# Attention stage of a diffusion block: bias and half of the rotary on GpSimd, softmax's small steps for two heads at once, a pair's scores three projection steps later

## The chip, the core and the metric

The program runs on one core of one Trainium2 chip. The metric is the device time of one execution in microseconds (us), the median of several runs. The engines are TensorE (PE; its weight loads are PEld), VectorE (DVE), ScalarE (ACT), GpSimd (POOL), and SyncE (SP), which issues all transfers. Each engine works through its own list of instructions in order.

## The reference

Two layers over 512 latent tokens (an 8 x 64 grid) and 256 context tokens, model width 1024, eight attention heads of 64. Cut to what the change touches:

```python
p, u, vs, q, k, v, gl = split(a @ w_in[l])            # one projection for everything
q, k = apply_rope(to_heads(q)), apply_rope(to_heads(k))   # x1*c - x2*s, x1*s + x2*c
# latent query: an 8 x 16 window of latent keys, and all context keys, in one softmax
s_win = einsum(q_row, k_win) * 64**-0.5 + rpb[:, dr][:, :, dc]
s_ctx = einsum(q_row, k_ctx) * 64**-0.5
p = softmax(concat([s_win, s_ctx]))
out = p_win @ v_win + p_ctx @ v_ctx
# in layer 0 the context tokens attend to the context tokens as well, without bias
```

Around it stand a pooling branch, a gating branch, three sigmoid gates, output projections and a squared-ReLU MLP. Only the latent stream of the last layer is returned.

## The kernel before

Everything is computed in fp32 accuracy: a tensor is split into a high part, rounded to a faster matmul type, and the low rest, and a product is three matmuls (high x high, high x low, low x high). So each weight tile of 128 x 1024 that a transfer brings is copied by ACT to a high part (L125) and subtracted by DVE to a low part (L119) before PE can use it. Three such tiles are kept ready.

Inputs stand with channels on partitions and tokens along the row. One output tile of the input projection (`proj`, matmuls at L429) is 128 channels, which is a pair of heads, by 512 latent and 256 context columns. It takes eight steps of six matmuls: three of 512 and three of 256 columns.

The attention stage goes pair by pair, four pairs to a layer. `stream` is the list of projection steps: for pair p the tiles of v, k and q, and after the fourth pair six gate tiles. When a tile is done a routine empties it from PSUM: `v_in` for v, and for k and q `rope_in`. The latter copies four groups of 32 partitions crosswise (ACT, `cp` at L125, 32x512), multiplies the product by the cosine (DVE, L122, PSUM source), the crosswise copy by the sine (DVE, L122, both sources in SBUF), adds the two (DVE, L116), and splits the sum into high (ACT) and low part (DVE, L119). Only then can the pair's scores be computed from it.

The loop over pairs mixes two kinds of PE work. A unit is 128 queries of one pair of heads: four latent units (`lat`) and in layer 0 two context units (`ctx`). Each unit runs

- `scores`: twelve matmuls of 64 rows (L662; six for `ctx`) to the one PSUM tile that is kept for scores; for each head a maximum over the context columns (DVE, L669), the addition of the bias with a running maximum (DVE, L672), the negated maximum (L674), the exponential with its sum (ACT, L675), the reciprocal (L678) and the product by it (L679);
- `turn`: transposes of the probabilities (PE, L691) to one of two PSUM tiles, emptied by ACT (high) and DVE (low);
- `values`: matmuls with v (L706) to the other of the same two PSUM tiles, emptied through an ACT copy and two DVE additions (L715, L716).

Between these, `fill` takes projection steps of the next pair from `stream`, so that PE has work while DVE and ACT are at the softmax. `stream` says HEAD after step HEADK of the next pair's v tile (counted from zero); there the filling holds until the pair before has all its projections, and then the pair's first scores come. `bias_load` brings the pair's 16 pieces of the bias table (16 transfers at L633), and `bias_make` builds from it and the mask six tables (two heads, three kinds of columns; L644, DVE). The table buffer exists once, so one kind can be rewritten only after the last unit that adds it.

A scheduler orders each engine's list by its own estimates; the order it made is shown below where it matters.

Of the kernel before, what the change touches and what calls it, by code (L numbers as in the profile page):

```python
# [10 lines left out]
AF = mybir.ActivationFunctionType  # L11
# [6 lines left out]
NL = 512  # L18
# [18 lines left out]
NCOLS = 140  # L37
HEADK = 4
CTXW = 0.5
# [56 lines left out]
def build(nc, tc, d, sb, ps):  # L96
# [309 lines left out]
    for l in range(2):  # L406
# [204 lines left out]
        def rope_in(p, which, o):  # L611
            nn, rings = (N, kring) if which == "k" else (n, qring)
            hi, lo = rings[0].next(), rings[1].next()
            xs, t1 = xsr.next(), t1r.next()
            for g in range(4):
                gg = g ^ 1
                cp(xs.f[32 * g:32 * g + 32, :], o[32 * gg:32 * gg + 32, 0:NL])
            mul(t1.f, o[:, 0:NL], cosb.f)
            if nn == N:
                cp(hi.r[:, NL:N], o[:, NL:N])  # L620
                sub(lo.r[:, NL:N], o[:, NL:N], hi.f[:, NL:N])
            mul(xs.f, xs.f, sinb.f)
            add(t1.f, t1.f, xs.f)
            split(hi, lo, t1.f)
            qk[p, which] = (hi, lo)
# [22 lines left out]

        def scores(p, kind, qt):
# [15 lines left out]
            m_ = sm.next().f  # L665
            pr = prr.next().f.rearrange("q (h x) -> q h x", h=2)
            for hh in range(2):
                top, neg, tot, inv_ = (m_[:, 5 * hh + i:5 * hh + i + 1] for i in range(1, 5))
                V.tensor_reduce(out=top, in_=s3[:, hh, w - 256:w], axis=AX.X, op=ALU.max)  # L669
                if kind == "lat":  # L670
                    top0, top = top, m_[:, 5 * hh:5 * hh + 1]
                    V.tensor_tensor_reduce(out=s3[:, hh, 0:256], in0=s3[:, hh, 0:256], in1=tabs[p][:, hh, BTYPE[qt], :],  # L672
                                           scale=1.0, scalar=top0, op0=ALU.add, op1=ALU.max, accum_out=top)
                V.tensor_scalar(out=neg, in0=top, scalar1=-0.125, scalar2=None, op0=ALU.mult)  # L674
                S.activation(out=pr[:, hh, 0:w], in_=s3[:, hh, 0:w], func=AF.Exp, bias=neg, scale=0.125, accum_out=tot)  # L675
# [395 lines left out]
```

## Time and profile before

| | |
|---|---|
| median of 3 runs | 1963.25 us (1963.22 to 1963.85) |
| span of the profiled execution | 1961.2 us |
| PE busy | 1920.1 us, 98% |
| PE weight loads busy | 1655.9 us, 84% |
| DVE busy | 1157.3 us, 59% |
| ACT busy | 781.4 us, 40% |
| POOL busy | 1.1 us, 14 instructions, all memsets |
| granted PE clock | 0.997 of full speed |

The span runs from the first to the last instruction of the profiled execution; that execution's own time is not given apart from it, and the median of the runs is 2.05 us above the span. A busy share of PE counts the time from a matmul's start to its modelled end; matmuls overlap, so a wait shorter than one matmul's own duration doesn't show as idle time.

### The profile page before, as it was taken

To read this page: it belongs to the slowest core of one execution; us is meant where nothing else is said; L and a number is where in the kernel's file an instruction comes from. 1 tells how busy PE (TensorE), PEld (TensorE's weight loads), DVE (VectorE), ACT (ScalarE), POOL (GpSimd) and SP (SyncE) were. 2 spreads that over 40 slices of the span, in tenths; PEclk is the share of its full clock that TensorE was granted. 3 is DMA by queue.
4 is the path that set the end of the run, shared out by engine and by line. 5 is a ranking of instruction groups with operands and counts; after the bars stand their busy time and mean duration, and the time that the engine had idled before them with its cause. 6 is when DMAs were issued, how large, how long until landed. Compare 5 with 4: busy or idle time off the path is not lost. (4 is left out here: it accounts for less than half of the span.)

```text
span 1961.2 us, 27925 instructions
## 1 busy us (share of the span) xinstructions
PE 1920.1 (98%) x11298; PEld 1655.9 (84%) x11298; DVE 1157.3 (59%) x2065; ACT 781.4 (40%) x1197; POOL 1.1 (0%) x14
## 2 busy tenths in 40 slices
PE   7999999999999999999999999999999999999998
PEld 3887778888888888888888898777888898989898
DVE  5759886755554656644444476888633554434356
ACT  5546664112143422413314454656322443424253
POOL 0000000000000000000000000000000000000000
PEclk9999999999999999999999999999999999999999
DMA  8231111433341433333433233211222222222224
GB/s 317 78 93 44 43 44 55 151 129 123 128 137 54 130 128 121 124 123 128 129 129 129 88 131 124 65 51 46 82 97 98 97 89 97 88 96 97 97 95 132
DMA packets 63440, 206.25 MB, mean 105 GB/s; under 512 B 7888, under 2 KB 14032, under 8 KB 63312
## 3 DMA queue, kind: packets, MB, share of 16 engines
q1 hardware_dynamic: 63312, 204.48, 31.8%
q8 instruction: 89, 1.46, 0.3%
q14 instruction: 39, 0.32, 0.1%
HBM read 202.35 MB, written 2.10 MB: 104 GB/s over the span
## 5 line engine op out<-in xcount | busy, mean ns | idle before, releaser
L224 PE MATMUL psum<-arena_r 128*128 128x512 f32 (+1 forms) x8016 | 1368.2, 333 | 0.0
L224 PEld LDWEIGHTS psum<-arena_r 128*128 128x128 f32 x8016 | 1209.7, 188 | 156.9 <-DVE arena_r L119 0.4
L125 ACT ACTIVATE arena_r<-arena_f 128x1024 fp32r<-128x1024 f32 (+4 forms) x393 | 371.8, 950 | 975.8 <-PE psum L224 805.2
L119 DVE TENSOR_TENSOR arena_r<-arena_f,arena_r 128x1024 fp32r<-128x1024 f32 (+4 forms) x393 | 425.2, 1085 | 254.0 <-ACT arena_r L125 245.9
L429 PE MATMUL psum<-arena_r 128*128 128x512 f32 x1776 | 369.5, 355 | 0.0
L429 PEld LDWEIGHTS psum<-arena_r 128*128 128x128 f32 x1776 | 282.6, 188 | 42.7 <-DVE arena_r L119 0.2
L871 DVE SCALAR_TENSOR_TENSOR arena_f<-psum,arena_f 128x512 f32<-128x512 f32 (+1 forms) x128 | 78.2, 632 | 256.2 <-PE psum L224 256.0
L250 DVE SCALAR_TENSOR_TENSOR arena_f<-arena_f 128x1024 bf16<-128x1024 f32 x128 | 156.3, 1221 | 1.4
L923 DVE COPY arena_f<-psum 128x2 f32<-128x2 f32 x64 | 10.2, 160 | 187.0 <-PE psum L224 187.0
L125 ACT ACTIVATE arena_f<-psum 64x128 f32<-64x128 f32 (+5 forms) x183 | 87.8, 490 | 60.0 <-PE psum L706 32.3
L116 DVE TENSOR_TENSOR arena_f<-arena_f 128x512 f32<-128x512 f32 (+8 forms) x119 | 80.9, 681 | 17.3 <-ACT arena_f L261 13.9
L125 ACT ACTIVATE arena_r<-psum 128x512 fp32r<-128x512 f32 (+2 forms) x108 | 58.2, 550 | 46.5 <-PE psum L691 29.7
L119 DVE TENSOR_TENSOR arena_r<-psum,arena_r 128x512 fp32r<-128x512 f32 (+2 forms) x108 | 67.2, 624 | 12.4 <-ACT arena_r L125 11.8
L122 DVE TENSOR_TENSOR arena_f<-psum,arena_f 128x512 f32<-128x512 f32 (+1 forms) x80 | 63.3, 791 | 6.7 <-ACT arena_f L125 6.5
L926 ACT ACTIVATE arena_f<-arena_f 128x512 f32<-128x512 f32 x96 | 59.3, 650 | 11.3 <-DVE arena_f L122 11.3
L675 ACT ACTIVATE arena_f<-psum,arena_f 128x512 f32<-128x512 f32 (+1 forms) x80 | 51.5, 644 | 22.8 <-DVE arena_f L674 22.3
L662 PE MATMUL psum<-arena_r 64*128 64x256 f32 x432 | 51.3, 303 | 5.3 <-ACT arena_f L675 2.9
L662 PEld LDWEIGHTS psum<-arena_r 64*128 64x128 f32 x432 | 38.1, 185 | 20.1 <-issue 6.0
L691 PE MATMUL psum<-arena_f 128*128 128x128 f32 x288 | 45.6, 280 | 9.2 <-DVE arena_f L716 8.0
L842 DVE SCALAR_TENSOR_TENSOR arena_f<-arena_f,psum 128x768 f32<-128x768 f32 (+1 forms) x48 | 39.0, 819 | 19.7 <-PE psum L224 19.5
L691 PEld LDWEIGHTS psum<-arena_f 128*128 128x128 f32 x288 | 31.5, 141 | 21.2 <-ACT arena_r L125 7.9
L706 PE MATMUL psum<-arena_r 128*128 128x256 f32 x288 | 46.6, 290 | 2.6 <-DVE arena_f L716 1.1
(79 smaller groups left out, 713.9 us busy)
## 6 DMA issues: line engine op xcount, KB each, us to landing
arena_f<-in_w_ff SPq DMA_DIRECT2D x144, 512.0 KB
arena_f<-in_w_in SPq DMA_DIRECT2D x84, 512.0 KB
arena_f<-in_w_modT SPq DMA_DIRECT2D x80, 512.0 KB
arena_f<-in_w_mod SPq DMA_DIRECT2D x16, 512.0 KB
arena_f<-in_w_br SPq DMA_DIRECT2D x16, 512.0 KB
arena_f<-in_w_o SPq DMA_DIRECT2D x16, 512.0 KB
arena_f<-in_rpb SPq DMA_DIRECT2D x128, 30.6 KB
arena_f<-in_xt SPq DMA_DIRECT2D x8, 384.0 KB
```

What stands on the lines that cost most here:

```text
L116: V.tensor_tensor(out=o, in0=a, in1=b, op=ALU.add)
L119: return V.tensor_tensor(out=o, in0=a, in1=b, op=ALU.subtract)
L122: V.tensor_tensor(out=o, in0=a, in1=b, op=ALU.mult)
L125: S.activation(out=o, in_=a, func=AF.Copy)
L224: T.matmul(ps_out[:, c0:c1], a, b[:, c0:c1], start=(i == 0), stop=(i == 3 * n - 1))
L250: V.scalar_tensor_tensor(out=junk.f.bitcast(BF16), in0=r.f, scalar=1.0, in1=cb.f[:, s * D:(s + 1) * D], op0=ALU.mult, op1=ALU.mult, accum_ ...
L429: T.matmul(o[:, c0:c1], w[x][:, k, :], ax[k][y][:, c0:c1], start=(i == 0), stop=(i == 23))
L662: T.matmul(so[:, hh * 512 + c0:hh * 512 + c0 + 256], a.r[pr, qs], b.r[pr, ks], start=(j == 0), stop=(j == 2))
L675: S.activation(out=pr[:, hh, 0:w], in_=s3[:, hh, 0:w], func=AF.Exp, bias=neg, scale=0.125, accum_out=tot)
L691: T.transpose(x[:, j * P:(j + 1) * P], pr[:, hh, b * P:(b + 1) * P], ident.f)
L871: V.scalar_tensor_tensor(out=hv(k, c0, c1), in0=o[:, c0:c1], scalar=mcol(l, j, k, s), in1=hv(k, c0, c1), op0=ALU.mult, op1=ALU.add)
L926: S.activation(out=r.f[:, c0:c1], in_=r.f[:, c0:c1], func=AF.Relu, bias=b.f[:, s_:s_ + 1])
```

## The change

Four edits, all inside the attention stage of both layers.

1. `bias_make` runs on GpSimd: six additions of 256 columns instead of six DVE instructions. For that the factor 8 on the bias and the factor 0.125 at the exponential are gone, and q is scaled by 0.125 when it is emptied from PSUM.
2. Of `rope_in`, the multiplication by the sine and the addition are on GpSimd (512 columns each, all operands in SBUF); what reads PSUM stays on ACT and DVE.
3. The first maximum, the negation and the reciprocal are one instruction for both heads instead of two. Both exponentials now wait for both heads' maxima, and both products for both sums.
4. HEADK is 7 instead of 4: a pair's first scores stand three projection steps later.

```diff
-HEADK = 4
+HEADK = 7
...
+            sc = 1.0 if which == "k" else 0.125
...
-                cp(xs.f[32 * g:32 * g + 32, :], o[32 * gg:32 * gg + 32, 0:NL])
-            mul(t1.f, o[:, 0:NL], cosb.f)
+                S.activation(out=xs.f[32 * g:32 * g + 32, :], in_=o[32 * gg:32 * gg + 32, 0:NL], func=AF.Copy, scale=sc)
+            G.tensor_tensor(out=xs.f, in0=xs.f, in1=sinb.f, op=ALU.mult)
+            V.scalar_tensor_tensor(out=t1.f, in0=o[:, 0:NL], scalar=sc, in1=cosb.f, op0=ALU.mult, op1=ALU.mult)
...
-            mul(xs.f, xs.f, sinb.f)
-            add(t1.f, t1.f, xs.f)
+            G.tensor_tensor(out=t1.f, in0=t1.f, in1=xs.f, op=ALU.add)
             split(hi, lo, t1.f)
...
-                    V.scalar_tensor_tensor(out=tab4[:, hh, y, :].rearrange("q (a k) -> q a k", k=8), in0=view, scalar=8.0,
-                                           in1=mask.f[:, y * 256:(y + 1) * 256].rearrange("q (a k) -> q a k", k=8),
-                                           op0=ALU.mult, op1=ALU.add)
+                    G.tensor_tensor(out=tab4[:, hh, y, :].rearrange("q (a k) -> q a k", k=8), in0=view,
+                                    in1=mask.f[:, y * 256:(y + 1) * 256].rearrange("q (a k) -> q a k", k=8), op=ALU.add)
...
+            V.tensor_reduce(out=two[0], in_=s3[:, :, w - 256:w], axis=AX.X, op=ALU.max)
...
+            V.tensor_scalar(out=two[2], in0=two[top], scalar1=-1.0, scalar2=None, op0=ALU.mult)
             for hh in range(2):
...
+                S.activation(out=pr[:, hh, 0:w], in_=s3[:, hh, 0:w], func=AF.Exp, bias=one[2][hh], accum_out=one[3][hh])
+            V.reciprocal(out=two[4], in_=two[3])
             for hh in range(2):
...
+                V.tensor_scalar(out=pr[:, hh, 0:w], in0=pr[:, hh, 0:w], scalar1=one[4][hh], scalar2=None, op0=ALU.mult)
```

The order on DVE at the first pair of layer 1, from the sine product of k to the first scores' maximum, before (L122 multiplies, L116 adds, L644 is the bias, L119 subtracts for a low part):

```order
L122 TENSOR_TENSOR arena_f<-arena_f 128x512
L116 TENSOR_TENSOR arena_f<-arena_f 128x512
L644 SCALAR_TENSOR_TENSOR arena_f<-arena_f 128x256 x6
L119 TENSOR_TENSOR arena_r<-arena_f,arena_r 128x512
L122 TENSOR_TENSOR arena_f<-arena_f 128x512
L122 TENSOR_TENSOR arena_f<-psum,arena_f 128x512
L119 TENSOR_TENSOR arena_r<-arena_f,arena_r 128x1024
L116 TENSOR_TENSOR arena_f<-arena_f 128x512
L119 TENSOR_TENSOR arena_r<-arena_f,arena_r 128x512
L669 TENSOR_REDUCE arena_f<-psum 128x1 x2
```

and in the changed kernel (L620 is the product with the cosine, L671 the maximum for both heads):

```order
L623 SCALAR_TENSOR_TENSOR arena_r<-psum,arena_r 128x256
L119 TENSOR_TENSOR arena_r<-arena_f,arena_r 128x512
L119 TENSOR_TENSOR arena_r<-arena_f,arena_r 128x1024
L620 SCALAR_TENSOR_TENSOR arena_f<-psum,arena_f 128x512
L119 TENSOR_TENSOR arena_r<-arena_f,arena_r 128x512
L119 TENSOR_TENSOR arena_r<-arena_f,arena_r 128x1024
L671 TENSOR_REDUCE arena_f<-psum 128x2
L675 ISA psum,arena_f<-psum,arena_f 128x256
```

The bias, two sine products and two sums are no longer between k's emptying and q's low part. On GpSimd, which had only memsets, the same place and the next pair's now read (L619 sine product, L625 sum, L646 bias):

```order
L619 TENSOR_TENSOR arena_f<-arena_f 128x512
L625 TENSOR_TENSOR arena_f<-arena_f 128x512
L646 TENSOR_TENSOR arena_f<-arena_f 128x256 x6
L619 TENSOR_TENSOR arena_f<-arena_f 128x512
L625 TENSOR_TENSOR arena_f<-arena_f 128x512
L646 TENSOR_TENSOR arena_f<-arena_f 128x256 x4
L619 TENSOR_TENSOR arena_f<-arena_f 128x512
L625 TENSOR_TENSOR arena_f<-arena_f 128x512
L646 TENSOR_TENSOR arena_f<-arena_f 128x256 x2
```

The rows are k, all six tables and q of the first pair, then four tables of the second pair ahead of its k, and the last two, which wait for the last latent unit of the first pair, ahead of its q. (In layer 0 the first pair's tables stand behind its q.)

The softmax of the second unit of layer 1 on DVE before:

```order
L669 TENSOR_REDUCE arena_f<-psum 128x1 x2
L672 ISA psum,arena_f<-psum,arena_f 128x256
L672 ISA arena_f 128x1
L672 ISA psum,arena_f<-psum,arena_f 128x256
L672 ISA arena_f 128x1
L674 TENSOR_SCALAR arena_f<-arena_f 128x1
L119 TENSOR_TENSOR arena_r<-psum,arena_r 128x4x128
L674 TENSOR_SCALAR arena_f<-arena_f 128x1
L119 TENSOR_TENSOR arena_r<-psum,arena_r 128x4x128
L678 RECIPROCAL arena_f<-arena_f 128x1
L679 TENSOR_SCALAR arena_f<-arena_f 128x512
L678 RECIPROCAL arena_f<-arena_f 128x1
L679 TENSOR_SCALAR arena_f<-arena_f 128x512
```

and now:

```order
L671 TENSOR_REDUCE arena_f<-psum 128x2
L675 ISA psum,arena_f<-psum,arena_f 128x256
L675 ISA arena_f 128x1
L675 ISA psum,arena_f<-psum,arena_f 128x256
L675 ISA arena_f 128x1
L119 TENSOR_TENSOR arena_r<-psum,arena_r 128x4x128
L677 TENSOR_SCALAR arena_f<-arena_f 128x2
L119 TENSOR_TENSOR arena_r<-psum,arena_r 128x4x128
L680 RECIPROCAL arena_f<-arena_f 128x2
L682 TENSOR_SCALAR arena_f<-arena_f 128x512 x2
```

Three of the small instructions are gone, and the reciprocal stands behind both heads' exponentials.

On SP, the bias pieces of the second pair of layer 0 and the weight loads (L205) around them, before:

```order
L205 DMA arena_f<-in_w_in 128x1024 [waits DMAHW2_49,DVE_49]
L205 DMA arena_f<-in_w_in 128x1024 [waits DMAHW3_49,DVE_49]
L205 DMA arena_f<-in_w_in 128x1024 [waits DMAHW4_49,DVE_49]
L633 DMA arena_f<-in_rpb 8x2x489 [waits DMAHW5_49,DVE_49]
L633 DMA arena_f<-in_rpb 8x2x489 [waits DMAHW6_49]
```

and now:

```order
L205 DMA arena_f<-in_w_in 128x1024 [waits DMAHW2_49,DVE_49]
L205 DMA arena_f<-in_w_in 128x1024 [waits DMAHW3_49,DVE_49]
L635 DMA arena_f<-in_rpb 8x2x489 [waits DMAHW4_49,Pool_49]
L635 DMA arena_f<-in_rpb 8x2x489 [waits DMAHW5_49]
L635 DMA arena_f<-in_rpb 8x2x489 [waits DMAHW6_49]
```

The pieces wait for GpSimd's tables instead of DVE's, and one weight load that stood ahead of the 16 pieces stands behind them.

## Rows read from the trace of the kernel before

**Rows 1.** Windows, both attention stages and two steady stretches: start:end, length, busy per engine (x instructions), clock, DMA.

```profile
124.00:320.00 196.00, 188.72 (x1218) 155.79 (x1217) 166.89 (x473) 119.32 (x261) 0.00 (x0) 1.00 0.17 52
1226.00:1392.00 166.00, 156.29 (x958) 127.54 (x958) 142.75 (x375) 103.10 (x208) 0.00 (x0) 1.00 0.18 55
1440.00:1480.00 40.00, 40.00 (x178) 33.14 (x177) 16.35 (x18) 10.41 (x14) 0.00 (x0) 1.00 0.27 92
1680.00:1720.00 40.00, 40.00 (x335) 40.00 (x334) 17.73 (x28) 20.11 (x27) 0.00 (x0) 1.00 0.28 93
```

**Rows 2.** Layer 0 attention (124 to 320), PE groups: count, busy, mean ns, idle before.

```profile
L429 PE MATMUL psum<-arena_r 128*128 128x512 f32 x320 | 118.9, 407 | 0.0
...
L662 PE MATMUL psum<-arena_r 64*128 64x256 f32 x240 | 28.8, 306 | 1.7 <-DVE arena_r L119 0.8 <-ACT arena_r L125 0.6 <-ACT arena_f L675 0.3
...
L691 PE MATMUL psum<-arena_f 128*128 128x128 f32 x156 | 25.0, 281 | 3.1 <-DVE arena_f L716 2.3 <-ACT arena_f L675 0.4 <-DVE arena_f L679 0.3
```

**Rows 3.** Layer 1 attention (1226 to 1392), the same PE groups.

```profile
L429 PE MATMUL psum<-arena_r 128*128 128x512 f32 x342 | 104.9, 401 | 0.0
...
L662 PE MATMUL psum<-arena_r 64*128 64x256 f32 x192 | 22.5, 300 | 3.6 <-ACT arena_f L675 2.6 <-ACT arena_r L125 1.0
...
L691 PE MATMUL psum<-arena_f 128*128 128x128 f32 x128 | 19.7, 279 | 6.0 <-DVE arena_f L716 5.8
```

**Rows 4.** Waits of ACT, layer 0 stage, then layer 1: us in total, times, longest.

```profile
ACT arena_f L675 <- DVE arena_f L674: 8.1, 14, 1.0
...
ACT arena_f L675 <- DVE arena_f L674: 14.2, 14, 2.0
```

**Rows 5.** Layer 0 attention, DVE groups by form.

```profile
L669 DVE TENSOR_REDUCE arena_f<-psum 128x1 f32<-128x256 f32 x48 | 19.5, 417 | 3.3 <-PE psum L662 2.8
...
L119 DVE TENSOR_TENSOR arena_r<-arena_f,arena_r 128x1024 fp32r<-128x1024 f32 x13 | 15.9, 1223 | 5.7 <-ACT arena_r L125 5.6
...
L644 DVE SCALAR_TENSOR_TENSOR arena_f<-arena_f 128x256 f32<-128x256 f32 x24 | 14.0, 621 | 0.1
...
L678 DVE RECIPROCAL arena_f<-arena_f 128x1 f32<-128x1 f32 x48 | 7.5, 158 | 4.5 <-ACT arena_f L675 3.8
...
L674 DVE TENSOR_SCALAR arena_f<-arena_f 128x1 f32<-128x1 f32 x48 | 6.8, 145 | 0.4
...
L122 DVE TENSOR_TENSOR arena_f<-arena_f 128x512 f32<-128x512 f32 x8 | 5.5, 684 | 0.0
```

**Rows 6.** Timeline at the first pair of layer 1: start, length, engine, line [idle].

```profile
1230.32 3.33 DVE L644 SCALAR_TENSOR_TENSOR arena_f<-arena_f 128x256 f32<-128x256 f32 x6
...
1231.16 2.44 ACT L125 ACTIVATE arena_f<-psum 32x512 f32<-32x512 f32 x4
...
1237.22 0.63 ACT L125 ACTIVATE arena_r<-arena_f 128x512 fp32r<-128x512 f32 x1 [2.54 <-DVE arena_f L116]
...
1237.90 0.51 PE L662 MATMUL psum<-arena_r 64*128 64x256 f32 x4 [1.01 <-ACT arena_r L125]
```

**Rows 7.** Groups: GpSimd in the whole program, and one ACT form.

```profile
L543 POOL MEMSET arena_f<- 128x16 f32 x4 | 0.4, 113 | 17.4 <-PE psum L337 12.3 <-DVE arena_f L285 3.0 <-DVE arena_r L119 2.1
...
L492 ACT ACTIVATE arena_f<-psum,arena_f 128x512 f32<-128x512 f32 x1 | 1.3, 1272 | 1.3 <-PE psum L490 1.3
```

**Rows 8.** Timeline, one unit's scores in layer 1.

```profile
1299.38 0.86 PE L662 MATMUL psum<-arena_r 64*128 64x256 f32 x10
```

**Rows 9.** Timeline, SP queue and one ACT weight copy, layer 0.

```profile
131.83 0.33 SPq L205 DMA_DIRECT2D arena_f<-in_w_in  x1
...
138.60 5.41 SPq L633 DMA_DIRECT2D arena_f<-in_rpb  x16
...
187.81 1.05 ACT L125 ACTIVATE arena_r<-arena_f 128x1024 fp32r<-128x1024 f32 x1
```

**Rows 10.** Timeline, end of a unit's softmax and its transposes, layer 0.

```profile
149.75 0.49 DVE L679 TENSOR_SCALAR arena_f<-arena_f 128x512 f32<-128x512 f32 x1
...
152.33 0.66 PE L691 MATMUL psum<-arena_f 128*128 128x128 f32 x4
```

More of the change, by code (lines that the diff above doesn't have):

```diff
@@ L616, in rope_in @@
                 gg = g ^ 1
[L617 to L618 removed]
+                S.activation(out=xs.f[32 * g:32 * g + 32, :], in_=o[32 * gg:32 * gg + 32, 0:NL], func=AF.Copy, scale=sc)
+            G.tensor_tensor(out=xs.f, in0=xs.f, in1=sinb.f, op=ALU.mult)
+            V.scalar_tensor_tensor(out=t1.f, in0=o[:, 0:NL], scalar=sc, in1=cosb.f, op0=ALU.mult, op1=ALU.mult)
             if nn == N:
[L620 to L623 removed]
+                S.activation(out=hi.r[:, NL:N], in_=o[:, NL:N], func=AF.Copy, scale=sc)
+                V.scalar_tensor_tensor(out=lo.r[:, NL:N], in0=o[:, NL:N], scalar=sc, in1=hi.f[:, NL:N],
+                                       op0=ALU.mult, op1=ALU.subtract)
+            G.tensor_tensor(out=t1.f, in0=t1.f, in1=xs.f, op=ALU.add)
             split(hi, lo, t1.f)
@@ L666, in scores @@
             pr = prr.next().f.rearrange("q (h x) -> q h x", h=2)
-            for hh in range(2):
[L668 to L675, printed above, removed]
+            two = [m_[:, 2 * i:2 * i + 2] for i in range(5)]
+            one = [[t[:, hh:hh + 1] for hh in range(2)] for t in two]
+            top = 0
+            V.tensor_reduce(out=two[0], in_=s3[:, :, w - 256:w], axis=AX.X, op=ALU.max)
+            if kind == "lat":
+                top = 1
+                for hh in range(2):
+                    V.tensor_tensor_reduce(out=s3[:, hh, 0:256], in0=s3[:, hh, 0:256], in1=tabs[p][:, hh, BTYPE[qt], :],
+                                           scale=1.0, scalar=one[0][hh], op0=ALU.add, op1=ALU.max, accum_out=one[1][hh])
+            V.tensor_scalar(out=two[2], in0=two[top], scalar1=-1.0, scalar2=None, op0=ALU.mult)
+            for hh in range(2):
+                S.activation(out=pr[:, hh, 0:w], in_=s3[:, hh, 0:w], func=AF.Exp, bias=one[2][hh], accum_out=one[3][hh])
+            V.reciprocal(out=two[4], in_=two[3])
             for hh in range(2):
-                tot, inv_ = (m_[:, 5 * hh + i:5 * hh + i + 1] for i in (3, 4))
-                V.reciprocal(out=inv_, in_=tot)
-                V.tensor_scalar(out=pr[:, hh, 0:w], in0=pr[:, hh, 0:w], scalar1=inv_, scalar2=None, op0=ALU.mult)
+                V.tensor_scalar(out=pr[:, hh, 0:w], in0=pr[:, hh, 0:w], scalar1=one[4][hh], scalar2=None, op0=ALU.mult)
             return pr, w
```

## The prediction

> **What bounds the kernel now.** I read the page first: PE is busy for 1920.1 of 1961.2 us, so only stretches in which PE gives something away can be won. The windows show where. In steady stretches PE issues 178 matmuls of 512 columns in 40 us, or 335 of 256 columns [rows 1], that is 0.2247 and 0.1194 us each. Layer 0's attention stage (124 to 320) took 196 us for 1218 matmuls, 320 of them of 512 columns [rows 1, 2]. At these rates 320 x 0.2247 + 898 x 0.1194 = 179 us would do, so at least 17 us are lost. Layer 1's stage (1226 to 1392) took 166 us for 958 matmuls, 342 of them wide [rows 1, 3]: 342 x 0.2247 + 616 x 0.1194 = 150 us, so at least 16 are lost. The scores' matmuls go faster than that, ten in 0.86 us [rows 8], about (0.86 - 0.30) / 9 = 0.06 us each when the last one's own 0.30 [rows 3] is taken off; for their 432 that makes another 25 us. So 33 to 58 us are lost in the two stages, and 7.3 + 9.7 = 17 us of it are seen as idle PE (196 - 188.7, 166 - 156.3) [rows 1]. The clock is 1.00 in every one of these windows: it is waiting, not the clock.
>
> Who is waited for? In the PE groups, the transposes wait 2.3 and 5.8 us for L716 [rows 2, 3]: that DVE addition empties the PSUM tile which `turn` wants next. The scores wait 0.8 + 0.6 + 1.0 us for L119 and L125, the low and high part of q at a pair's start, and 0.3 + 2.6 us for the exponentials (L675) of the unit before, with 0.4 at the transposes [rows 2, 3]. The exponentials themselves waited 8.1 + 14.2 us for the negated maximum on DVE [rows 4]. All of this points at DVE's queue: DVE is busy 166.9 of 196 us and 142.8 of 166 us there, 85 and 86%, ACT 61 and 62% [rows 1].
>
> **What the change removes from DVE.** In layer 0: 24 bias instructions of 0.621 us, 14.9; eight sine products of 0.684, 5.5; eight sums that I take at the same price, 5.5; and for 24 units one negation (0.145) and one reciprocal (0.158), 3.5 + 3.8 [rows 5]. Two maxima of 0.417 become one of twice the columns. No row has that one; its price lies between 0.42 and 0.83, and I take 0.69, so 24 x 0.14 = 3.4. Together 36.6 us, and DVE falls from 166.9 to 130, 66% of the stage. Layer 1 has 16 units instead of 24: 14.9 + 11 + 16 x 0.45 = 33 us, 142.8 to 110, again 66%. The product with the cosine stays one PSUM instruction, and ACT's copies are as many as before; I cost the scale in them at nothing: it adds no instruction, so there is nothing to hide.
>
> **What it puts on GpSimd.** Per layer 16 instructions of 512 and 24 of 256 columns. The trace has only memsets there, 0.11 us for 16 columns [rows 7]; the dearest plain pass over 512 columns on any engine is ACT's strided 1.27 us [rows 7]. Between these ends I take 1.2 for 512 columns, near the upper, because the instruction does the same work as one, and 0.8 for 256. The Trainium skill (GPSIMD Engine Reference, Performance versus the Vector engine) gives 4.50 us for an addition of 2048 columns, 1.1 us as an estimate for 512; by it the sums below would not change. Per layer that is 16 x 1.2 + 24 x 0.8 = 38 us in 166 or more, so GpSimd's queue is no bound; at the upper end 1.27 for all forty it would be 51.
>
> **A pair's start.** The tightest is layer 1's first pair. Before, q's four crosswise copies ended at 1233.6, the sum was late behind 3.33 us of bias, the high part came at 1237.2, and the scores began at 1237.9 after 1.01 us of idle PE [rows 6]. Now the scores stand three steps later. A step is 3 x (0.2247 + 0.1194) = 1.03 us, so PE reaches them at about 1237.9 - 1.0 + 3.1 = 1240.0. On GpSimd k's two instructions, six tables and q's two stand in a row, 4 x 1.2 + 6 x 0.8 = 9.6 us. k's copies end one q tile before q's (24 matmuls of 512 columns, 5.4 us), at 1228.2, so q's sum is done at 1237.8, its high part 0.63 later [rows 6], its low part, at the price of DVE's other 512-column instructions of 0.68 [rows 5], at 1239.1. It is in time by 0.9 us. Were GpSimd's ten instructions a tenth dearer, PE would wait again, at this one place. The later pairs have 8 steps, 8.2 us, between q's last matmul and the scores, with at most two tables in between. So the whole 2.4 us of idle PE at the starts go. The three steps themselves are not lost: they are matmuls that come earlier instead of later.
>
> **Transfers.** The bias pieces now wait for GpSimd's tables, and one weight load stands behind the 16 pieces that was ahead of them. It was issued at 131.83, and the pieces took 5.41 us from 138.60 [rows 9]. Tables that end some 2 us later than now and 5.4 us of pieces put this load at about 146. With four buffers in turn it is copied at 187.81 [rows 9], the fourth copy after its issue, so 40 us cover it: nothing.
>
> **The units.** Fewer instructions stand ahead of L716 and of the negation. DVE's spare time goes from 14 to 34%; I take 60% of the 8.1 us of waits for L716, 4.9, and 40% of the 3.3 us for exponentials, 1.3, since there the single scores tile stays. Of the loss not seen as idle, at least 33 - 17 = 16 us, I take 15%, 2.4. Against that stands the pairing. Both exponentials wait for the second head's maximum, and the first product for the second sum, which puts the first product one exponential later. A unit's chain from scores to the last product grows by 0.3 to 0.4 us. In the unit at 150 the last product ended at 150.24 and its transposes began at 152.33 [rows 10], 2.1 us of cover, so most units pay nothing; over 40 units I allow 2 us.
>
> **Sum.** -2.4 - 4.9 - 1.3 - 2.4 + 2 = -9.0 us. The profiled span of 1961.2 becomes 1952.2. The median of the runs is 2.05 us above the span, so the time is **1954 us**, 0.5% faster. A measurement of this kernel tells about 0.2%, 4 us, from no change.
>
> **Rivals.**
> *Slower, GpSimd against DVE at the unit's end.* If a GpSimd instruction and a DVE instruction that reads SBUF get in each other's way, the one that comes second stands still for up to a whole instruction of 1.2 us, and the products (0.49 us [rows 10]), the weight splits (1.22 [rows 5]) and the low parts are such. It decides when a unit's chain grows by more than its cover of about 2.1 us [rows 10]. Pairing takes 0.4 of that; one weight split and two products, caught by a whole instruction each, make it 0.4 + 3 x 1.2 = 4.0, which is 1.9 us over. From five such units of 40 on (9.5 us) the gain is eaten; in a quarter of them it is 10 x 1.9 = 19 us, 1961.2 - 9 + 19 + 2 = 1973. For it: nothing in this trace, since no GpSimd instruction that reads SBUF is in it. Against it: GpSimd is busy for a fifth of the stage (38 of 196 us), so three meetings in one unit are rare. Just this is a rule of the Trainium skill (SBUF - State Buffer, Who interferes with whom): GpSimd's ports are DVE's second pair, held by one of them for a whole instruction, and a DVE instruction with two SBUF inputs, or in a two-port mode, contends. By that rule the meetings happen; no run here shows it yet. Chance 0.15.
> *No change, the waits move.* The PSUM tile for scores exists once, ACT works in order with 62%, and PE's next wait is for the exponential instead of L716. Then only the starts and a little are won: 1961.2 - 3 + 2 = 1960 to 1963. For it: the wait of the scores for L675 in layer 1, 2.6 us, is second to L716's 5.8 [rows 3]. Against it: that wait comes itself from DVE, 14.2 us [rows 4]. Chance 0.16.
> *More.* All 17 us of idle PE and a few of the hidden ones go: 1961.2 - 20 + 2 = 1943. For it: the scores stand in unbroken groups of twelve in most units now. Chance 0.17.
>
> **Chances and range.** The forecast has 0.52, with its own range 1948 to 1959 (half or one and a half of the gain). Faster by over 0.2%: 0.52 + 0.17 and a little of the second rival, 0.70; within 0.2%: 0.15; slower: 0.15. The range that holds 8 in 10 leaves out the far end of *more* and nearly all of the slower case: 1944 to 1965.
>
> **What would show it.** DVE busy in the two stages near 130 and 110 us. No idle PE at L663, the scores' line now, at a pair's start. Waits of the transposes for L719 (L716 before) under half of 8.1 us. GpSimd's groups at 0.8 and 1.2 us; if they are at twice that, layer 1's first pair waits about 9 us. If DVE instructions with SBUF sources grow longer than 1.22 and 0.49 us, or show idle time ahead of them that nothing ended, the first rival is at work. The forecast is wrong if PE's idle time in the stages stays near 17 us, or if it falls and the stages don't get shorter.

## The result, and the profile after

The changed kernel takes 1984.44 us (median of four runs, 1983.36 to 1987.06) against 1963.24: 1.1% slower, ratio 1.011 [1.0095, 1.0124]. I had forecast 1954. The profiled execution is one of 1987.06 us with a span of 1985.2, 24.0 above the span of before.

The page, its first lines:

```profile
span 1985.2 us, 27855 instructions
...
PE 1925.8 (97%) x11298; PEld 1663.5 (84%) x11298; DVE 1115.4 (56%) x1865; ACT 778.7 (39%) x1197; POOL 89.3 (4%) x94
```

Where the 24 us lie is told by when the PE reaches three places: the merge of layer 0, layer 1's first projection, the merge of layer 1. Timelines of PE, before and then after:

```profile
341.30 10.99 PE L224 MATMUL psum<-arena_r 128*128 128x512 f32 x61
...
1165.49 5.40 PE L429 MATMUL psum<-arena_r 128*128 128x512 f32 x23
...
1400.81 29.54 PE L224 MATMUL psum<-arena_r 128*128 128x512 f32 x129
```

```profile
351.70 0.51 PE L224 MATMUL psum<-arena_r 128*128 128x512 f32 x2
...
1181.28 4.04 PE L429 MATMUL psum<-arena_r 128*128 128x512 f32 x17
...
1424.58 15.71 PE L224 MATMUL psum<-arena_r 128*128 128x512 f32 x68
```

So 10.4 us are lost up to the first merge, 5.4 more between the two layers' attention, where the change touches nothing (the last section comes back to these), and 8.0 more up to the second merge. The windows that answer to [rows 1] show the two stages (start:end, length, PE, PEld, DVE, ACT and POOL busy, granted clock, DMA):

```profile
124.00:330.00 206.00, 186.68 (x1224) 157.96 (x1223) 143.80 (x356) 116.83 (x257) 44.67 (x40) 0.98 0.15 47
...
215.00:220.00 5.00, 2.24 (x12) 1.98 (x13) 4.00 (x13) 2.00 (x6) 1.70 (x2) 0.88 0.11 27
220.00:225.00 5.00, 5.00 (x30) 4.21 (x29) 2.68 (x6) 1.80 (x5) 0.00 (x0) 0.78 0.37 84
1226.00:1410.00 184.00, 167.75 (x1020) 138.76 (x1020) 121.59 (x286) 105.32 (x211) 43.51 (x40) 0.98 0.18 58
```

Layer 0's stage now needs 206 us for 1224 matmuls, before 196 for 1218 [rows 1], and idle PE grew from 7.3 to 206 - 186.7 = 19.3 us. DVE is less busy (143.8 and 121.6 us, where 130 and 110 were forecast), and yet the PE waits more. The waits of the whole program (us in total, times, longest):

```profile
ACT arena_r L125 <- POOL arena_f L625: 34.6, 16, 5.0
...
DVE arena_f L680 <- ACT arena_f L679: 29.0, 28, 2.9
...
PE psum L694 <- DVE arena_f L719: 19.7, 14, 3.1
...
PE psum L709 <- DVE arena_r L119: 5.9, 11, 0.8
...
PE psum L663 <- ACT arena_r L125: 3.5, 2, 1.8
```

The transposes' wait for the addition L719 stood at 8.0 us in the whole trace of before (2.3 + 5.8 in the two stages [rows 2, 3]). At the head stands a wait that has doubled: all 16 high copies of q and k on ACT wait for GpSimd's sum, 34.6 us. Before, 15 of them waited for DVE's sum, 9.1 + 7.6 = 16.7 us. The rows of the two stages of before:

```profile
ACT arena_r L125 <- DVE arena_f L116: 9.1, 7, 2.0
...
ACT arena_r L125 <- DVE arena_f L116: 7.6, 8, 2.5
```

What doubled with it is DVE's idle time ahead of its low parts of 512 columns, which stand behind high copies, in the whole program, before and then after:

```profile
L119 DVE TENSOR_TENSOR arena_r<-arena_f,arena_r 128x512 fp32r<-128x512 f32 x68 | 46.6, 689 | 30.4 <-ACT arena_r L125 29.4 <-PE psum L662 0.9
```

```profile
L119 DVE TENSOR_TENSOR arena_r<-arena_f,arena_r 128x512 fp32r<-128x512 f32 x68 | 46.7, 690 | 58.9 <-ACT arena_r L125 58.9
```

GpSimd's groups:

```profile
L646 POOL TENSOR_TENSOR arena_f<-arena_f 128x256 f32<-128x256 f32 x48 | 45.3, 964 | 119.4 <-DVE arena_f L675 114.0 <-DVE arena_f L677 4.7
...
L625 POOL TENSOR_TENSOR arena_f<-arena_f 128x512 f32<-128x512 f32 x16 | 22.4, 1402 | 1.3
L619 POOL TENSOR_TENSOR arena_f<-arena_f 128x512 f32<-128x512 f32 x16 | 20.7, 1292 | 201.5 <-ACT arena_f L618 201.5
```

One such wait, from the timeline of one tile in layer 0 (L618 crosswise copies, L619 and L625 GpSimd's product and sum, L718 and L719 the additions):

```profile
207.92 1.80 ACT L618 ACTIVATE arena_f<-psum 32x512 f32<-32x512 f32 x3
...
209.86 1.31 POOL L619 TENSOR_TENSOR arena_f<-arena_f 128x512 f32<-128x512 f32 x1 [4.31 <-ACT arena_f L618]
...
211.11 1.23 DVE L119 TENSOR_TENSOR arena_r<-arena_f,arena_r 128x1024 fp32r<-128x1024 f32 x1 [0.34 <-ACT arena_r L125]
211.25 2.24 POOL L625 TENSOR_TENSOR arena_f<-arena_f 128x512 f32<-128x512 f32 x1
...
213.52 0.63 ACT L125 ACTIVATE arena_r<-arena_f 128x512 fp32r<-128x512 f32 x1 [2.14 <-POOL arena_f L625]
...
214.19 0.69 DVE L119 TENSOR_TENSOR arena_r<-arena_f,arena_r 128x512 fp32r<-128x512 f32 x1 [1.85 <-ACT arena_r L125]
214.79 0.28 DVE L718 TENSOR_TENSOR arena_f<-psum,arena_f 64x128 f32<-64x128 f32 x1
...
215.59 0.28 DVE L719 TENSOR_TENSOR arena_f<-psum,arena_f 64x128 f32<-64x128 f32 x1
...
215.96 0.27 ACT L125 ACTIVATE arena_f<-psum 64x128 f32<-64x128 f32 x1 [1.19 <-DVE arena_f L719]
...
217.31 0.30 DVE L719 TENSOR_TENSOR arena_f<-psum,arena_f 64x128 f32<-64x128 f32 x1
...
217.76 0.63 PE L694 MATMUL psum<-arena_f 128*128 128x128 f32 x4 [3.06 <-DVE arena_f L719]
```

Read it from the top. GpSimd's two instructions end at 213.49. ACT stands 2.14 us at the high copy, DVE 1.85 us at the low part behind it. The addition L718, whose PSUM tile was ready, is queued behind that low part; the copy at 215.96, which the second half of the same tile needs, has to wait for its only buffer, and so the tile comes free at 217.61 and the transposes begin 3.06 us late. The tile is one of the two with the longest sum: 2.24 and 2.25 us, where the other 14 sums took 1.26 to 1.29; in 13 of those 14 tiles ACT waits for 1.1 to 5.0 us all the same.

The clock fell with it: the windows 215:220 and 220:225 above were granted 0.88 and 0.78, stretches partly at 1.2 instead of 2.4 GHz, behind that pause; before, 1.00 all through [rows 1]. It is a part of the price: four windows of 40 us (200:240, 240:280, 1240:1280 and 1320:1360) were granted 0.96, so the slower clock itself took up to 4 x 40 x 0.04 = 6.4 us, an estimate, of the 18.4 us lost in the two stages.

### The profile page after: what moved, and what is told of

It is laid out like the page before. It is cut to its first block, busy times and chain, and to the rows that moved or that the text cites. A ratio compares the mean times of both kernels' runs of the same rounds, so it can differ in the third digit from the quotient of the medians.

```text
span 1985.2 us, 27855 instructions
## 1 busy us (share of the span) xinstructions
PE 1925.8 (97%) x11298; PEld 1663.5 (84%) x11298; DVE 1115.4 (56%) x1865; ACT 778.7 (39%) x1197; POOL 89.3 (4%) x94
## 4 chain that ended last, share of the span: by engine, by line
PE 84%; DVE 5%; ACT 5%; POOL 2%; issue 2%; DMA 1%; SPq 0%; POOLq 0%; DVEq 0%; ACTq 0%
PE psum L224 69%; PE psum L429 9%; ACT arena_r L125 2%; DVE arena_r L119 2%; ACT arena_f L618 1%; ACT arena_f L679 1%; PE psum L709 1%; PE psum L381 1%; PE psum L694 1%; DMA arena_f<-in_w_mod 1%; PE psum L663 1%; POOL arena_f L625 1%; POOL arena_f L619 1%; DVE psum L675 1%; POOL arena_f L646 1%
## 5 line engine op out<-in xcount | busy, mean ns | idle before, releaser
L224 PEld LDWEIGHTS psum<-arena_r 128*128 128x128 f32 x8016 | 1212.5, 189 | 159.4 <-ACT arena_f L782 0.5
L119 DVE TENSOR_TENSOR arena_r<-arena_f,arena_r 128x1024 fp32r<-128x1024 f32 (+4 forms) x393 | 426.4, 1087 | 287.2 <-ACT arena_r L125 279.1
L429 PEld LDWEIGHTS psum<-arena_r 128*128 128x128 f32 x1776 | 286.8, 191 | 43.0 <-issue 0.2
L116 DVE TENSOR_TENSOR arena_f<-arena_f 128x768 f32<-128x768 f32 (+8 forms) x103 | 70.0, 681 | 16.7 <-ACT arena_f L261 13.3
L125 ACT ACTIVATE arena_f<-psum 64x128 f32<-64x128 f32 (+5 forms) x119 | 49.9, 435 | 73.1 <-PE psum L709 33.2
L119 DVE TENSOR_TENSOR arena_r<-psum,arena_r 128x512 fp32r<-128x512 f32 (+2 forms) x96 | 62.0, 653 | 14.8 <-ACT arena_r L125 13.7
L125 ACT ACTIVATE arena_r<-psum 128x512 fp32r<-128x512 f32 (+2 forms) x96 | 53.3, 571 | 36.7 <-PE psum L694 26.3
L694 PE MATMUL psum<-arena_f 128*128 128x128 f32 x288 | 44.0, 279 | 20.5 <-DVE arena_f L719 19.7
L709 PEld LDWEIGHTS psum<-arena_r 128*128 128x128 f32 x288 | 39.8, 195 | 17.6 <-DVE arena_r L119 11.5
L663 PE MATMUL psum<-arena_r 64*128 64x256 f32 x432 | 46.3, 306 | 6.2 <-ACT arena_r L125 3.5
L122 DVE TENSOR_TENSOR arena_f<-psum,arena_f 128x768 f32<-128x768 f32 (+1 forms) x64 | 52.2, 816 | 0.0
## 6 DMA issues: line engine op xcount, KB each, us to landing
arena_f<-in_rpb SPq DMA_DIRECT2D x128, 30.6 KB
```

The lines of the kernel that those rows point to most:

```text
L116: V.tensor_tensor(out=o, in0=a, in1=b, op=ALU.add)
L119: return V.tensor_tensor(out=o, in0=a, in1=b, op=ALU.subtract)
L125: S.activation(out=o, in_=a, func=AF.Copy)
L224: T.matmul(ps_out[:, c0:c1], a, b[:, c0:c1], start=(i == 0), stop=(i == 3 * n - 1))
L429: T.matmul(o[:, c0:c1], w[x][:, k, :], ax[k][y][:, c0:c1], start=(i == 0), stop=(i == 23))
L663: T.matmul(so[:, hh * 512 + c0:hh * 512 + c0 + 256], a.r[pr, qs], b.r[pr, ks], start=(j == 0), stop=(j == 2))
```

## The experiments

**Queue theory:** what costs is the high copy's place on ACT. ACT and DVE work their lists in order, and stand at the high copy and the low part while the copies and additions behind these could run. **Port theory** (the rival of the forecast): GpSimd's SBUF reads hold DVE up. **Pairing theory:** the pairing of the two heads makes everything wait for the later one. Ratios are to the kernel before in the same set of runs.

### Each part alone, and the rotary taken back

*no_rope*: the changed kernel with the sine product and the sum on DVE again.

```diff
-G.tensor_tensor(out=xs.f, in0=xs.f, in1=sinb.f, op=ALU.mult)
...
-G.tensor_tensor(out=t1.f, in0=t1.f, in1=xs.f, op=ALU.add)
+mul(xs.f, xs.f, sinb.f)
+add(t1.f, t1.f, xs.f)
```

> The changed kernel with the rotary's sine product and sum back on DVE; bias on GpSimd, pairing and HEADK 7 stay. Queue theory (the high copy of q and k stands at the head of ACT's list until GpSimd's sum is done, and the copies that empty PSUM stand behind it): the 34.6 us of ACT waits for L625 and most of the 19.7 us of transposes waiting for L719 go, 1955 to 1966 us. Port theory (GpSimd and DVE hinder each other): 24 of 40 GpSimd instructions of a layer stay, so most of the loss stays, above 1975. Pairing theory (both heads' exponentials and products wait for each other): nearly all of it stays, 1978 to 1985.

1959.97 us, ratio 0.9979 [0.9969, 0.9989]: the loss is gone, as the queue theory had it and the two others had not.

*rope_only*: the kernel before with that same swap the other way round, and nothing else of the change.

> The kernel before with the sine product and the sum of the rotary on GpSimd, nothing else changed (HEADK 4). Queue theory: 16 waits of ACT of some 2 us each as in the changed kernel, and less lead at a pair's start, 1975 to 1990 us. Port theory: about two fifths of the loss, 1965 to 1975. Pairing theory: about 1963 or faster.

1969.99 us, 1.0037 [1.0024, 1.005]. Slower, but by a third of the loss only. This is a miss for the queue theory, which had 1975 or more, and within what the port theory had.

*pair_only* (before, with one maximum, negation and reciprocal for both heads) and *bias_only* (before, with the tables and the scale in q):

```diff
+V.tensor_reduce(out=two[0], in_=s3[:, :, w - 256:w], axis=AX.X, op=ALU.max)
...
+V.tensor_scalar(out=two[2], in0=two[top], scalar1=-0.125, scalar2=None, op0=ALU.mult)
...
+V.reciprocal(out=two[4], in_=two[3])
```

> The kernel before with the maximum, the negation and the reciprocal for two heads at once, nothing else changed. Queue and port theory: no GpSimd work, so within 5 us of 1963 us. Pairing theory: 1975 to 1985, with DVE idle in front of the reciprocal.

```diff
-V.scalar_tensor_tensor(out=tab4[...], in0=view, scalar=8.0, in1=mask.f[...], op0=ALU.mult, op1=ALU.add)
+G.tensor_tensor(out=tab4[...], in0=view, in1=mask.f[...], op=ALU.add)
```

> The kernel before with the bias tables on GpSimd (and the scale moved to q for that), nothing else changed: 48 GpSimd instructions of about 0.96 us, none of which ACT waits for. Queue theory: 30 us less on DVE and no wait added, 1950 to 1963 us. Port theory: half of all GpSimd time is here, 1970 to 1978. Pairing theory: 1955 to 1963.

1961.39 us, 0.999 [0.9979, 1.0001], and 1957.11 us, 0.9969 [0.9958, 0.9981]. Neither costs; the bias on GpSimd wins 5.9 us, against the port theory's 1970 or more. So the rotary is the cause, and something in its company triples its price.

### Load without a wait, and a wait taken off ACT

*ghost*: *no_rope* with four GpSimd instructions of 256 columns per q and k tile, whose result nobody reads.

```diff
+for c in (0, 256):
+    G.tensor_tensor(out=sp.f, in0=hi.f[:, c:c + 256], in1=sinb.f[:, c:c + 256], op=ALU.mult)
+    G.tensor_tensor(out=sp.f, in0=hi.f[:, c:c + 256], in1=cosb.f[:, c:c + 256], op=ALU.add)
```

> The changed kernel with the rotary's sine product and sum back on DVE, and in their place four GpSimd instructions of 256 columns per q and k tile (product and sum of the finished high part with the sine and cosine tables, two SBUF inputs each) into a buffer that nobody reads: GpSimd's load stays, nobody waits for it. Queue theory (ACT's waiting high copy is what costs): as the kernel without GpSimd's rotary, 1955 to 1962 us. Port theory (GpSimd's SBUF reads slow DVE down): at least half of the loss comes back, 1970 or more, with DVE's products, low parts and weight splits longer by tenths of a microsecond on average.

1963.64 us, 0.9988 [0.9975, 1.0001]. GpSimd was busier than in the changed kernel (100.2 against 89.3 us), and 20 us of the loss are still absent. That is 3.7 us above *no_rope* (1.8 by the ratios), with intervals that overlap; no more than about 4 us of this load's price belongs to the ports. Its instructions lie beside other DVE work than the rotary's, so *rope_q3* below, with the rotary's own, is the closer test.

*rope_all_g*: the changed kernel with the high copy and the low subtraction on GpSimd as well.

```diff
-split(hi, lo, t1.f)
+G.tensor_copy(out=hi.r[:, 0:NL], in_=t1.f)
+G.tensor_tensor(out=lo.r[:, 0:NL], in0=t1.f, in1=hi.f[:, 0:NL], op=ALU.subtract)
```

> The changed kernel with the rotary's high copy and low subtraction on GpSimd too, so that no instruction of ACT or DVE waits for GpSimd's sum; the chain from copies to low part gets longer by about 1.5 us per tile. Queue theory: ACT's 34.6 us of waits for the sum go, the additions that empty the transposes' tile come in time, 1955 to 1968 us, with some idle PE at the scores of a pair's start. Port theory: GpSimd does twice the SBUF work, so 1984 or more.

1966.89 us, 1.0011 [0.9999, 1.0022]: 17.5 us come back with 120.2 us of GpSimd work. Its waits:

```profile
PE psum L695 <- DVE arena_f L720: 6.0, 12, 1.0
...
PE psum L664 <- POOL arena_r L626: 4.1, 1, 4.1
```

The transposes wait 6.0 instead of 19.7 us; the longest wait left among these is that of the scores at one pair's start, 4.1 us behind GpSimd's longer chain. Both results speak for the queue theory and against the ports.

### What triples the price

*no_bias* (the changed kernel, bias tables on DVE), *no_head* (`HEADK = 4`) and *no_pair* (small steps per head as before) each undo one companion, with the diffs of the parts the other way round.

> The changed kernel with the bias tables back on DVE (rotary half on GpSimd, pairing and later scores stay). Queue theory: GpSimd's sum no longer stands behind bias tables, ACT's waits for it fall from 34.6 towards the 25 us of the rotary alone, and the time to 1968 to 1974 us. If the loss beyond the rotary alone comes from the scores' later place or from the pairing, it stays at 1980 or more.

> The changed kernel with the scores of a pair at the fourth projection step again. Queue theory: ACT's waits for GpSimd's sum hit a stretch of the same density, so the time stays at 1980 to 1988 us, or gets worse by up to 5 us, since the scores wait for the late high part. If the three steps' move is what packs the copies, the additions and the waiting high copy together, the time falls to 1968 to 1974 us, as the rotary alone.

> The changed kernel without the pairing of the two heads' small steps (rotary half and bias on GpSimd, scores three steps later). If the pairing makes the rotary dear (both exponentials and then DVE's reciprocal stand behind the waiting high copy): 1964 to 1972 us. If the loss comes from the rotary and the later scores whatever the pairing does: 1976 or more.

1981.38 us, 1.008 [1.0057, 1.0103]; 1976.23, 1.0058 [1.0035, 1.008]; 1982.4, 1.008 [1.0052, 1.0108]. *no_bias* misses what the queue theory had, and *no_head* lies between its two expectations: neither the tables ahead of the sum on GpSimd nor the pairing is what makes the rotary dear; pairing theory falls. Putting the scores back gives some 8 of the 14 us above *rope_only*; the other 6 are of the size of a doubt that the last section names, and which edit they come from stays open.

What the kernels with the sum on GpSimd differ in is seen in ACT's lists. Between a tile's last crosswise copy and its high copy (the first pair left out) there stand, in layer 0 and layer 1: in *rope_only* 5 to 7 and 2 to 4 instructions; in *no_head* 4 to 6 and 2 to 4; in *no_bias*, *no_pair* and the changed kernel 2 to 4 and 1 to 3. The shorter this cover, the slower these kernels; the waits for the sum (25.5, 28.3, 28.6, 37.6 and 34.6 us) follow it less closely. In the kernel before, with the sum on DVE, it is 5 to 9 and 3 to 7. Up to here the cover is argued, not shown, as the cause, and it can't be all: *head_only*, next, has 3 to 5 and 2 to 4 and is faster than the kernel before.

*head_only* (before, `HEADK = 7`) and *bias_pair* (*pair_only* and *bias_only* together):

> The kernel before with the scores three projection steps later and nothing else. If the later place wins the idle time at the pairs' starts, as predicted, 1959 to 1961 us. If it shifts the output projection of layer 0 into its slower spacing of matmuls (236 instead of 231.5 ns, seen so far in every profile with the later scores and in none without), 1964 to 1968 us, with no gain in the attention stages over 3 us.

> The kernel before with the bias tables on GpSimd and the pairing, scores at the fourth step, the whole rotary on DVE. Queue theory, with the gains that the two edits showed alone (5.9 and 1.6 us, in the two attention stages 6.6 and 5.3): 1950 to 1956 us, faster than both kernels. If the two gains are of the same waits, 1957 as the bias alone.

1957.82 us, 0.9966 [0.9953, 0.9979]: faster than either theory had it, and its merge runs at the quicker spacing, so the suspicion about `HEADK` falls. 1961.78 us, 0.9984 [0.997, 0.9998]: above both expectations; the gains of bias and pairing don't add, and the two together are no faster than the bias alone (1957.11).

### The copy's place, with GpSimd's work as it is

*rope_late*: the split is written four projection steps later.

```diff
-            split(hi, lo, t1.f)
+            late.append((hi, lo, t1.f))
...
+                    if i == LATE:
+                        flush()
```

> The changed kernel, all its edits and GpSimd's work as they are, but a tile's high copy on ACT and low part on DVE stand four projection steps later in the lists (about 4.1 us, against the 2.6 us that GpSimd's product and sum take), so that ACT and DVE come to them when the sum is there. Queue theory: ACT's waits for the sum fall from 34.6 to under 8 us, the transposes' waits for the additions from 19.7 to under 8 us, and the time to 1954 to 1964 us. Port theory, or any in which GpSimd's work itself is what costs: 1978 or more.

1980.77 us, 1.008 [1.0058, 1.0101], and no verdict, since the edit did not do what it says: the scheduler orders the lists by its own estimates and put the copy back, with the same counts of 2 to 4 and 1 to 2 ahead of it. The wait of its waits view and of the timeline that answers to the one above (all lines are one higher here):

```profile
ACT arena_r L126 <- POOL arena_f L626: 35.2, 16, 5.0
```

```profile
211.86 0.63 ACT L126 ACTIVATE arena_r<-arena_f 128x512 fp32r<-128x512 f32 x1 [2.14 <-POOL arena_f L626]
```

*rope_q3* and *rope_q5* fix the place: the split is queued behind the ACT instruction that was written last when four (six) more steps were written; this sets the order on the list and adds no wait.

```diff
 def flush():
     if late:
-        split(*late.pop())
+        acts = [i for i in nc.cur_bb.bb.instructions if i.engine == late[0][3]]
+        with tc.issue_after(acts[-1]):
+            split(*late.pop()[:3])
```

What this does to ACT's list at the tile of the timeline above, in the changed kernel and in *rope_q3* (`arena_r<-arena_f 128x512` is the high copy):

```
133 L618 ACTIVATE arena_f<-psum 32x512 x3
134 L622 ACTIVATE arena_r<-psum 128x256
135 L125 ACTIVATE arena_r<-arena_f 128x1024
136 L125 ACTIVATE arena_f<-psum 64x128
137 L125 ACTIVATE arena_r<-arena_f 128x512
138 L125 ACTIVATE arena_r<-psum 128x4x128
```

```
134 L619 ACTIVATE arena_f<-psum 32x512 x3
135 L623 ACTIVATE arena_r<-psum 128x256
136 L126 ACTIVATE arena_r<-arena_f 128x1024
137 L126 ACTIVATE arena_f<-psum 64x128 x2
138 L126 ACTIVATE arena_r<-psum 128x4x128 x2
139 L680 ACTIVATE arena_f<-psum,arena_f 128x512 x2
140 L126 ACTIVATE arena_r<-arena_f 128x512
```

> The changed kernel, all its edits and GpSimd's work as they are, with the high copy queued on ACT behind the ACT instruction that was written last when four more projection steps had been written. In the order made this puts 4 to 8 ACT instructions between the last crosswise copy and the high copy in layer 0's later pairs and 3 to 5 in layer 1's, against 2 to 4 and 1 to 2 in the changed kernel. Queue theory: ACT's waits for GpSimd's sum fall from 34.6 to under 15 us, the transposes' from 19.7 to under 10, and the time to 1958 to 1968 us. If GpSimd's work itself costs, or the late low part: 1978 or more.

> The same, queued behind what was written after six steps: 8 to 11 ACT instructions in layer 0 and 3 to 8 in layer 1. Queue theory: ACT's waits at the sum under 12 us; the high copy may now be late for the scores one or two steps later, so 1957 to 1970 us. If GpSimd's work itself costs: 1978 or more.

1958.07 us, 0.9961 [0.9946, 0.9976], and 1961.24 us, 0.9974 [0.9963, 0.9984]. 26 and 23 us come back, GpSimd's instructions untouched; some 5 of the 26 may be the pace of a later stage (last section). ACT's waits in *rope_q5* are 12.2 us, just above the 12 that were expected at most. The same place in *rope_q3*'s timeline, and its waits:

```profile
204.78 1.80 ACT L619 ACTIVATE arena_f<-psum 32x512 f32<-32x512 f32 x3
...
206.71 1.30 POOL L620 TENSOR_TENSOR arena_f<-arena_f 128x512 f32<-128x512 f32 x1 [4.32 <-ACT arena_f L619]
...
208.09 2.24 POOL L626 TENSOR_TENSOR arena_f<-arena_f 128x512 f32<-128x512 f32 x1
...
209.10 0.28 DVE L719 TENSOR_TENSOR arena_f<-psum,arena_f 64x128 f32<-64x128 f32 x1
...
211.73 0.63 PE L695 MATMUL psum<-arena_f 128*128 128x128 f32 x4 [1.01 <-DVE arena_f L720]
...
214.58 0.62 ACT L126 ACTIVATE arena_r<-arena_f 128x512 fp32r<-128x512 f32 x1
```

```profile
ACT arena_r L126 <- POOL arena_f L626: 14.5, 8, 5.0
...
PE psum L695 <- DVE arena_f L720: 6.4, 12, 1.0
```

GpSimd's sum is as slow as before (2.24 us), but DVE's addition runs at 209.10 while the sum is still being made, the transposes begin after 1.01 us of idle PE in place of 3.06, and the high copy at 214.58 waits for nothing. The eight waits that are left, 14.5 us, hold the longest one, 5.0, which stands at layer 1's first pair, where the edit moves nothing.

The edit moves the high copy on ACT and the low part on DVE together, and the scheduler then placed some other entries of ACT's, DVE's and PE's lists differently too. So what is shown is the price of the split's place, and no run separates ACT's part of it from DVE's. *bias_head*, the fastest kernel of the next section, speaks for DVE's. DVE makes the sum there; at the same tile ACT has three instructions as cover, as in the changed kernel, and waits almost as long:

```profile
209.95 0.28 DVE L716 TENSOR_TENSOR arena_f<-psum,arena_f 64x128 f32<-64x128 f32 x1
210.06 0.63 ACT L125 ACTIVATE arena_r<-arena_f 128x512 fp32r<-128x512 f32 x1 [1.77 <-DVE arena_f L116]
...
210.73 0.69 DVE L119 TENSOR_TENSOR arena_r<-arena_f,arena_r 128x512 fp32r<-128x512 f32 x1
...
213.05 0.63 PE L692 MATMUL psum<-arena_f 128*128 128x128 f32 x4 [1.07 <-DVE arena_f L717]
```

But DVE does not stand still for the low part: the addition L716 is ahead of it in DVE's list, and the transposes wait 1.07 us. DVE's idle time ahead of its low parts of 512 columns was 30.6 us in this kernel, 31.3 in *no_rope*, 42.2 in *rope_q3*, against the 58.9 of the changed kernel.

### Do the harmless parts add up?

*bias_head* is *bias_only* with `HEADK = 7`; *no_pair_q3* is *rope_q3* without the pairing.

> The kernel before with the bias tables on GpSimd and the scores three steps later, no pairing, the whole rotary on DVE. If the gains that the two edits showed alone (5.9 and 6.7 us) add up: 1950 to 1953 us, the best of all. If the two remove the same waits (the scores at a pair's start behind the bias on DVE): 1955 to 1958.

> The changed kernel without the pairing, with the high copy queued behind what ACT was given in four further projection steps. Without the queueing this kernel took 1982.4 us. Queue theory: 1952 to 1960 us, the same step of more than 20 us as with the pairing; whether it also beats the version with the whole rotary on DVE (1953.8) tells if GpSimd's half of the rotary is worth anything once nobody stands waiting for it: below 1952 yes, above 1955 no.

1953.79 us, 0.9936 [0.992, 0.9952], the best of all, and 1954.92 us, 0.9955 [0.9941, 0.997]. The gains of bias and later scores nearly add (5.9 + 6.7 against 11.2). The second time lies between its two marks, 1952 and 1955: no gain of GpSimd's half of the rotary over DVE's is seen, and a small one is not ruled out. The fixed place is worth 27 us without the pairing too (1982.4 to 1954.9; here too some 5 may be the later stage's pace).

## Why the prediction was wrong, step by step

**The step that failed is "The units".** It counted that "fewer instructions stand ahead of L716 and of the negation" and took 60% of the 8.1 us of waits away. It priced the rotary's move by what leaves DVE and by GpSimd's durations, and asked who waits for the sum at one place only, a pair's start. It did not name the waiting instruction's followers: the high copy on ACT and the low part on DVE stand in the middle of lists whose next entries empty the PSUM tiles. The term that I gave as -4.9 us is +11.7 (8.0 to 19.7). *rope_q3* shows it: with another place for the split, and GpSimd's instructions as they were, that wait is 6.4 us and the kernel is 0.4% faster than before. The order that the forecast was based on could be read: 2 to 4 ACT instructions between copies and high copy in layer 0 and 1 to 2 in layer 1, where GpSimd's two take 2.6 us or more. Of the other terms there, the PE's waits for exponentials (-1.3 in the sum) went from 3.3 to 2.4 us; no row measures the -2.4 for the loss that was not seen as idle.

**GpSimd's prices** were too low by 8 to 20%: 1.29 and 1.40 us where I took 1.2, 0.96 where I took 0.8, 88.4 us in all where I had 76; the 1.1 us that the prediction cites as an estimate is lower still. The mean of the sum is that high because two of the sixteen lie beside DVE's weight split, one of them the 2.24 us in the timeline above; the other 14 cost what the product does, as the 1.26 below. **A pair's start**: I had written that at a tenth dearer the PE would wait at layer 1's first pair. It does, as the timeline there shows:

```profile
1246.45 6.48 POOL L646 TENSOR_TENSOR arena_f<-arena_f 128x256 f32<-128x256 f32 x6
...
1254.26 1.26 POOL L625 TENSOR_TENSOR arena_f<-arena_f 128x512 f32<-128x512 f32 x1
...
1255.56 1.58 ACT L125 ACTIVATE arena_r<-arena_f 128x512 fp32r<-128x512 f32 x2 [4.98 <-POOL arena_f L625]
...
1256.24 1.31 PE L663 MATMUL psum<-arena_r 64*128 64x256 f32 x6 [1.78 <-ACT arena_r L125]
```

Six tables at 1.08 us each push q's sum back; 1.78 us of idle PE stand where 1.01 stood [rows 6]. The 2.4 us that I expected here did not come: the scores' waits for q went from 2.4 to 3.7 us. That the later place itself was a gain is shown by *head_only*, 6.7 us, more than I gave it; only 0.6 us of these waits are left there.

**DVE** fell, but by 41.9 us of busy time where I had 36.6 + 33. Two reasons are seen, worth some 9 of the 28 us; the rest was not broken down. The means of [rows 5] overlap: six bias instructions of 0.621 us took 3.33 us in a row [rows 6], 0.555 each. And the paired negation takes 0.281 us, nearly two single ones:

```profile
L671 DVE TENSOR_REDUCE arena_f<-psum 128x2 f32<-128x512 f32 x40 | 27.3, 683 | 1.6 <-PE psum L663 1.2
...
L677 DVE TENSOR_SCALAR arena_f<-arena_f 128x2 f32<-128x2 f32 x40 | 11.2, 281 | 0.6
```

The paired maximum is 0.683, where I took 0.69. **Transfers**: nothing, right (ACT's waits for `in_w_in` are 1.7 us in both kernels). **Pairing**: +2 in the sum. Alone it gained 1.6 us, within its interval of no change. In company it may cost a little: *rope_q3* and *no_pair_q3* are 3 us apart against it (1.2 by their ratios, with intervals that overlap), *no_rope* and *bias_head* 6 (8 by their ratios), of which some 5 may be the pace of the last section. Two waits grow with it: DVE's reciprocal waited for the second exponential for 24.2 us in *no_rope* and 3.3 in *bias_head*, and the matmuls of `values` for the low part of the probabilities for 5.9 us in the changed kernel and 1.0 in *no_pair*. A slip in the forecast's own range: one and a half of the gain ends at 1950, not at 1948.

**The rivals.** The slower one had the right sign and the wrong mechanism; *ghost* leaves it no more than about 4 us. DVE's weight splits in layer 0's stage went from 1.22 to 1.25 us, and the products stayed at 0.48. None of the rivals was the one that happened.

## What to carry to other kernels

When an operation moves to another engine, price the instruction that waits for it by what stands behind it in its own list, on every engine that stays: here 2.7 us per tile on GpSimd cost 24 us, because ACT and DVE stood in front of work that was ready. Read in the order how many instructions lie between the last producer and the first consumer, and compare their time with the new chain's; and where a scheduler makes the order, an edit that only writes something later can leave the list as it was, so look at the list, not at the code.

## What was not expected of the hardware

**Layer 0's merge has two paces.** Windows of its matmuls (400 to 440 us, no instruction of it changed), before and then after:

```profile
400.00:440.00 40.00, 40.00 (x233) 35.00 (x232) 1.00 0.40 128
```

```profile
400.00:440.00 40.00, 40.00 (x228) 34.70 (x227) 1.00 0.37 119
```

233 or 228 matmuls in 40 us at the same clock, from the merge's start until the next stage: 5.4 of the 24.0 us between the two profiled executions. The slower pace (228 or 229) also stands in the profiles of *no_rope*, *ghost*, *rope_all_g*, *no_bias*, *no_pair*, *rope_late* and *rope_q5*, the quicker one (232 or 233) in those of all other kernels here, *rope_q3*, *no_pair_q3*, *bias_head* and *head_only* among them. Single runs of one kernel lie as far apart and further (*no_rope* 1954.1 and 1961.6); as one execution of each was profiled, no run shows whether by the same pace. What sets the pace was not found, so differences of 5 us between two of the kernels here carry that doubt. The rotary's price doesn't: *no_rope* has the slower pace like the changed kernel, and its span is 25.5 us shorter.

**GpSimd and DVE do slow each other**, at a small price. GpSimd's sum took 2.24 us beside DVE's 1.23 us weight split, which had begun 0.14 us ahead of it, and 1.26 alone. The two-column negation had a mean of 0.161 us in *pair_only*, where GpSimd has only memsets, and 0.281 in the changed kernel: 0.15 to 0.17 in the 25 that no GpSimd instruction overlaps, up to 0.89 in the 15 others. The Trainium skill (SBUF - State Buffer, Who interferes with whom) says that the two share a pair of ports which one holds for its whole instruction. The trace agrees that such instructions get longer; at the weight split GpSimd was the one that came second. Of the effect on the kernel *ghost* leaves no more than about 4 us, and *rope_q3*, with sums of 2.13 to 2.25 us at three tiles, is faster than the kernel before.
